# Split SiLU gate, 16 tiles through one core: fifteen stores moved from ScalarE's DMA queue to GpSimd's, with eight rows in one packet

## The chip, the cores and the metric

The kernel runs on one core of one Trainium2 chip. The metric is device time in microseconds (us) of the program; lower is better. The core has one set of 16 DMA engines, which move all data between device memory and the on-chip buffer, and five instruction engines, of which this kernel uses four: ScalarE (ACT in the profile), VectorE (DVE), GpSimd (POOL) and SyncE (SP). TensorE does nothing here.

## The reference

The input has 32 x 512 rows of 2048 float32. Each row is cut in two halves; the first half goes through SiLU and is multiplied by the second.

```python
def reference(x):
    half_dim = x.shape[-1] // 2
    x1, x2 = x[..., :half_dim], x[..., half_dim:]
    silu_x1 = x1 * (1 / (1 + np.exp(-x1)))
    return (silu_x1 * x2).astype(np.float32)
```

So 134.22 MB are read, 67.11 MB are written, and each output element needs one activation and one product.

## The kernel before

The 16384 rows are cut into 16 tiles. A tile is 128 partitions times K = 8 rows of 2048 numbers, so a partition holds 64 KB of input (one contiguous stretch of memory) and 32 KB of output. Each of the 16 DMA engines serves 8 partitions of a tile. In the trace, a load of one tile is therefore 8 packets of 65,536 bytes on each engine, and a store of one tile 8 packets of 32,768 bytes on each engine. The text calls such a packet a row of the engine.

There are two input buffers (`in_pool`, tile `xt`) and two output buffers (`out_pool`, tile `ot`). The order of the instructions is written out by hand; no scheduler moves them.

- `load(i)` (L82) is issued by SP on its DMA queue, which the profile calls q1. `load(0)` and `load(1)` come first. `load(i + 2)` is written after the work of tile i, and has to wait until the product of tile i has read the buffer that it will overwrite.
- For tiles 0 to 14, ScalarE computes SiLU into `ot` (L86) and VectorE multiplies `ot` by the second half of `xt` (L93). Tile 0 is worked in four pieces of two columns (`KC_EDGE`), tiles 1 to 14 in one piece each.
- The store of a tile (L112) is issued by ScalarE on its own DMA queue, which the profile calls q10, once the product is done. For tile 0 it is five transfers, cut by partitions and columns (`OPENING`); for tiles 1 to 14 it is one.
- Tile 15 is worked in two halves (`KS`), each with its own SiLU and product, and its two half stores (L120) are issued by ScalarE.

SiLU of tile i writes the output buffer that tile i - 2 used, so it has to wait until the store of tile i - 2 has landed.

Of the kernel before, what the change touches and what calls it, by code (L numbers as in the profile page):

```python
# [1 line left out]

# [4 lines left out]


def issue_ahead_of_the_first_barrier(nc):

    head, body = nc.main_func.blocks[:2]
    load = next(ins for ins in body.instructions if type(ins).__name__ == "InstDMACopy")
    at = next(
        j for j, ins in enumerate(head.instructions)
        if ins.engine == load.engine and type(ins).__name__ == "InstDrain"
    )
    body.instructions = [ins for ins in body.instructions if ins.name != load.name]  # L20
    head.instructions = head.instructions[:at] + [load] + head.instructions[at:]


@with_exitstack
def kernel(
    ctx: ExitStack,
    tc: tile.TileContext,
    x: bass.AP,
    out: bass.AP,
):  # L30

    nc = tc.nc
    P = nc.NUM_PARTITIONS

    x_flat = x.flatten_outer_dims()  # L40
    out_flat = out.flatten_outer_dims()
    num_rows, in_cols = x_flat.shape
    half = in_cols // 2
    dt = x_flat.dtype

    K = 8
    KC_EDGE = 2
    KS = 4
    OPENING = [
        (slice(0, None, 4), slice(0, 2)),  # L50
        (slice(2, None, 4), slice(0, 4)),
        (slice(2, None, 4), slice(4, None)),
        (slice(0, None, 4), slice(2, None)),
        (slice(1, None, 2), slice(None)),
    ]
    PLAN = [K] * (num_rows // (P * K))

    in_pool = ctx.enter_context(tc.tile_pool(name="in_pool", bufs=2))
    out_pool = ctx.enter_context(tc.tile_pool(name="out_pool", bufs=2))

    plan = []
    row = 0
    for k in PLAN:
        plan.append((row, k))
        row += P * k
    assert row == num_rows
    n_tiles = len(plan)

    def view(flat, i):
        row0, k = plan[i]  # L70
        return flat[row0:row0 + P * k].rearrange("(p k) d -> p k d", k=k)

    nc.at_finalize(issue_ahead_of_the_first_barrier)


    ctx.enter_context(tc.manual_schedule())

    loaded = {}

    def load(i):  # L80
        xt = in_pool.tile([P, K, in_cols], dt, name="xt")
        nc.sync.dma_start(out=xt[:, :plan[i][1], :], in_=view(x_flat, i))  # L82
        loaded[i] = xt

    def silu(ot, xt, c, ce):
        nc.scalar.activation(  # L86
            out=ot[:, c:ce, :],
            in_=xt[:, c:ce, :half],
            func=mybir.ActivationFunctionType.Silu,
        )  # L90

    def mul(ot, xt, c, ce):
        nc.vector.tensor_mul(  # L93
            out=ot[:, c:ce, :],
            in0=ot[:, c:ce, :],
            in1=xt[:, c:ce, half:],
        )

    load(0)
    load(1)  # L100
    for i in range(n_tiles):
        xt = loaded.pop(i)
        ov = view(out_flat, i)
        ot = out_pool.tile([P, K, half], dt, name="ot")
        if i < n_tiles - 1:
            kc = KC_EDGE if i == 0 else K
            for c in range(0, K, kc):
                silu(ot, xt, c, c + kc)
                mul(ot, xt, c, c + kc)

            for ps, ks in OPENING if i == 0 else [(slice(None), slice(None))]:
                nc.scalar.dma_start(out=ov[ps, ks], in_=ot[ps, ks])  # L112
            if i + 2 < n_tiles:
                load(i + 2)
            continue
        for c in range(0, K, KS):
            silu(ot, xt, c, c + KS)
            mul(ot, xt, c, c + KS)
        for c in range(0, K, KS):
            nc.scalar.dma_start(out=ov[:, c:c + KS], in_=ot[:, c:c + KS])  # L120


# [1 line left out]
_INS = ['x']  # L124
_OUTS = [((32, 512, 1024), 'float32')]


# [23 lines left out]
```

## Time and profile before

| | |
|---|---|
| time, median of 3 runs | 470.35 us (470.28, 470.35, 472.34) |
| span of the profiled execution, first to last instruction | 468.4 us |
| that execution's own time | not recorded; the median is 1.95 us over the span |
| VectorE busy | 139.3 us in 20 instructions (30%) |
| ScalarE busy | 114.1 us in 21 instructions (24%) |
| GpSimd busy | 0.2 us in 4 instructions |
| moved by DMA | 201.33 MB at a mean of 430 GB/s |

The page of a profile gives the busy time of each engine, the span cut into 40 slices with the busy share of the 16 DMA engines in each, the DMA queues, and the chain of work that ended last, followed back from the last instruction. Other views list the instructions in order of time, or the busy time in stretches of the span that one chooses. The trace also holds a record of every DMA packet: queue, size, start and duration. "DMA out_dram<-ot" is a store, "DMA xt<-in_x_dram" a load. A DMA "lands" when its last semaphore increment arrives.

### The profile page before, as it was taken

How to read it: one execution, taken by the hardware profiler on the slowest of the kernel's cores; microseconds unless marked ns; L12 is line 12 of the kernel's file. 1: busy time of each engine (PE TensorE's matmuls, PEld its weight loads, DVE VectorE, ACT ScalarE, POOL GpSimd, SP SyncE). 2: the span in 40 equal slices, each digit the busy share in tenths (PEclk: the TensorE clock that was granted, in tenths of full speed). 3: DMA queues.
4: the chain of work that ended last, by engine and by line, in shares of the span. 5: the costliest groups of instructions: out<-in, count | busy, mean ns of one | idle time of the engine just before them, and what ended most of it. 6: DMA issues, size and time to landing. Idle time of an engine off the chain costs nothing.

```text
span 468.4 us, 185 instructions
## 1 busy us (share of the span) xinstructions
DVE 139.3 (30%) x20; ACT 114.1 (24%) x21; POOL 0.2 (0%) x4
## 2 busy tenths in 40 slices
DVE  0070600704207042070520605116061150602543
ACT  1142305005050050601406014060230602306060
POOL 0000000000000000000000000000000000000000
DMA  9899999999999999999999999899999899999998
GB/s 442 364 470 425 448 403 403 493 403 403 448 465 431 403 442 409 493 403 414 437 448 448 403 448 465 386 448 439 411 493 442 372 439 493 403 448 403 428 423 358
DMA packets 4880, 201.33 MB, mean 430 GB/s; under 512 B 592, under 2 KB 592, under 8 KB 592
## 3 DMA queue, kind: packets, MB, share of 16 engines
q1 hardware_dynamic: 2304, 134.22, 66.4%
q10 hardware_dynamic: 2576, 67.11, 33.2%
HBM read 134.22 MB, written 67.11 MB: 430 GB/s over the span
## 4 chain that ended last, share of the span: by engine, by line
DMA 72%; DVE 14%; ACT 11%; DVEq 1%; issue 0%
DMA out_dram<-ot 63%; DVE ot L93 14%; ACT ot L86 11%; DMA xt<-in_x_dram 9%; DVEq L146 1%
## 5 line engine op out<-in xcount | busy, mean ns | idle before, releaser
L93 DVE TENSOR_TENSOR ot<-ot,xt 128x8192 f32<-128x8192 f32 (+2 forms) x20 | 139.3, 6983 | 321.1 <-ACT ot L86 321.1
L86 ACT ACTIVATE ot<-xt 128x8192 f32<-128x8192 f32 (+2 forms) x20 | 112.8, 5661 | 340.2 <-DMA out_dram<-ot 305.8
L86 ACT ACT_TABLE_LOAD x1 | 1.3, 1283 | 0.8 <-PEq L135 0.8
L135 POOL MEMSET const-bfloat16-1.0<- 128x1 bf16 x1 | 0.1, 102 | 0.0
L135 POOL MEMSET const-uint8-127<- 128x1 uint8 x1 | 0.1, 102 | 0.0
L135 POOL MEMSET const-float32-1.0<- 128x1 f32 x1 | 0.1, 99 | 0.0
L135 POOL MEMSET const-float32-0.0<- 128x1 f32 x1 | 0.1, 98 | 0.2 <-issue 0.2
## 6 DMA issues: line engine op xcount, KB each, us to landing
out_dram<-ot ACTq DMA_DIRECT2D x14, 4096.0 KB, 42.2
out_dram<-ot ACTq DMA_DIRECT2D x3, 2048.0 KB, 6.9
out_dram<-ot ACTq DMA_DIRECT2D x2, 512.0 KB, 17.6
out_dram<-ot ACTq DMA_DIRECT2D x1, 768.0 KB, 28.2
xt<-in_x_dram SPq DMA_DIRECT2D x16, 35.1
out_dram<-ot ACTq DMA_DIRECT2D x1, 256.0 KB, 11.3
```

Of the source, the lines that this page charges most:

```text
L86: nc.scalar.activation(out=ot[:, c:ce, :], in_=xt[:, c:ce, :half], func=mybir.ActivationFunctionType.Silu,)
L93: nc.vector.tensor_mul(out=ot[:, c:ce, :], in0=ot[:, c:ce, :], in1=xt[:, c:ce, half:],)
L135: nc = _bacc.Bacc("TRN2", target_bir_lowering=False, num_devices=1)
L146: with _tile.TileContext(nc) as tc:
```

## The change

The stores of tiles 0 to 14 are issued by GpSimd in place of ScalarE, on GpSimd's own DMA queue. Each is one transfer of a whole tile, that of tile 0 too, so that `OPENING` goes. The argument `single_packet=True` asks that what one DMA engine gets of a transfer, here eight rows of 32 KB, be framed as one packet. The loads stay on SP, and the two half stores of tile 15 stay on ScalarE. No tile, buffer or computation changes.

```diff
     KS = 4
-    OPENING = [
-        (slice(0, None, 4), slice(0, 2)),
-        (slice(2, None, 4), slice(0, 4)),
-        (slice(2, None, 4), slice(4, None)),
-        (slice(0, None, 4), slice(2, None)),
-        (slice(1, None, 2), slice(None)),
-    ]
     PLAN = [K] * (num_rows // (P * K))
...
-            for ps, ks in OPENING if i == 0 else [(slice(None), slice(None))]:
-                nc.scalar.dma_start(out=ov[ps, ks], in_=ot[ps, ks])
+            nc.gpsimd.dma_start(out=ov, in_=ot, single_packet=True)
             if i + 2 < n_tiles:
                 load(i + 2)
             continue
```

Instruction by instruction, ScalarE loses 19 DMA issues and keeps 2, GpSimd gains 15 between its start and its end, each of which waits for the product of its tile, and SP's 16 loads stand in the same order with the same waits for the products.

## The prediction

> **What bounds the kernel now.** I read the page's slices and queues first.
>
> ```profile
> DMA  9899999999999999999999999899999899999998
> DMA packets 4880, 201.33 MB, mean 430 GB/s; under 512 B 592, under 2 KB 592, under 8 KB 592
> q1 hardware_dynamic: 2304, 134.22, 66.4%
> q10 hardware_dynamic: 2576, 67.11, 33.2%
> ```
>
> The reader is to see that the 16 DMA engines are busy 66.4% + 33.2% = 99.6% of the span, from the first slice to the last. VectorE (30%) and ScalarE (24%) wait most of the time. Then the chain that ended last:
>
> ```profile
> DMA 72%; DVE 14%; ACT 11%; DVEq 1%; issue 0%
> DMA out_dram<-ot 63%; DVE ot L93 14%; ACT ot L86 11%; DMA xt<-in_x_dram 9%; DVEq L146 1%
> ```
>
> The chain names compute for 25%, but the engines go on moving other tiles while it computes: it is a chain of releases, and the bound is the data. The packet records say the same: 8 rows of a load take 8 x 2.418 = 19.34 us on an engine, 8 rows of a store 8 x 1.213 = 9.70 us, and 16 x 29.04 = 464.7 us of the 468.4 us are rows. First packets start at 1.0 us, the last ends at 467.0 us. So nothing can be won but by shorter rows, and something is lost only where an engine has nothing to move. Where could that be? At the end. There I asked for stretches (columns: stretch, length, DVE, ACT, POOL, clock, DMA share, GB/s) and the order of time:
>
> ```profile
> 410.60:439.60 29.00, 8.69 (x1) 7.03 (x1) 0.00 (x0) 1.00 1.00 434
> 439.60:445.50 5.90, 0.00 (x0) 0.00 (x0) 0.00 (x0) 1.00 1.03 444
> 445.50:448.00 2.50, 0.00 (x0) 0.00 (x0) 0.00 (x0) 1.00 0.97 419
> 448.00:456.10 8.10, 4.44 (x2) 7.12 (x2) 0.00 (x0) 1.00 1.05 453
> ```
>
> ```profile
> 439.57 0.34 ACTq L112 DMA_DIRECT2D out_dram<-ot  x1
> 448.01 7.12 ACT L86 ACTIVATE ot<-xt 128x4096 f32<-128x4096 f32 x2 [17.20 <-DMA out_dram<-ot]
> 451.66 8.76 DVE L93 TENSOR_TENSOR ot<-ot,xt 128x4096 f32<-128x4096 f32 x2 [12.13 <-ACT ot L86]
> 456.12 4.67 ACTq L120 DMA_DIRECT2D out_dram<-ot  x2
> ```
>
> While the last tile is computed (448.0 to 456.1) DMA is full, because stores are late: the last load row of an engine ends at 443.6, and then 3 rows of store 13 and the 8 of store 14 are left, 11 x 1.213 = 13.3 us of work. This backlog hides tile 15's compute. It exists because the two queues take turns: in the packet records each engine alternates one load row, one store row, in a ratio of bytes of 2 to 1, which is that of the whole work, so both queues stay backlogged. Store 14 is issued at 439.57, and its last row ends at 456.9.
>
> **The change, part by part.**
>
> The 19 issues that ScalarE loses (338 to 633 ns each) lie in its idle time: it waits 305.8 us for stores and 34.4 us for loads. Worth nothing. If no queue ran dry, OPENING would be worth nothing either: tile 0's rows carry the same bytes, beside a load that is queued anyway; on an engine 12 rows become 8. The load of tile i + 2 is issued at the same event as before, the end of product i; SP holds no store, so no load moves behind one.
>
> Row length: 65,536 B take 2418 ns, 32,768 B 1213, 16,384 B 611. That is a line with 8 ns per row. If one packet saved all of it, 120 rows x 8 ns = 1.0 us; if rows had to be fetched in another way they could be longer. The nearest row is the trace's third kind of queue (code loading): 8192 B there take 307 ns at best, beside 309 ns on q10, though three of seven take 361 to 549. I take 1213 ns.
>
> The start of a transfer on GpSimd's queue, called d (issue to first row ready), is not in the trace. The nearest rows are 0.87 us (half store issued at 456.12, first row 457.00) and 1.0 us (first load). The low end is 0.87; the high end is unknown, and I carry 5 us, which is what the first store piece took under load (issue 26.02, rows at 31.04), most of it waiting for rows ahead of it. I take 1 to 2.5, nearer the idle rows. [...]
>
> The framing is the part that matters. If an engine takes turns by packet, its turn for a store is now 8 rows (9.70 us) against one load row (2.42): a store, once its turn comes, is done in one go, and the backlog at the end may be gone. The alternation of single rows above is the trace's own evidence for turns. [...]
>
> I follow one engine through this. From the first store (arrived about 26.9, began after the row 28.34 to 31.04, not at 28.34) I read that an engine has its next row chosen when a row starts.
>
> Tile 0: load 0's rows end at 21.0, product 0 at 32.6. Load 1's rows start at 21.0 + 2.42k, so its seventh at 35.5 and its eighth at 37.9. A store arriving before 35.5 (some engines 35.8) goes ahead of the eighth row. It arrives at 32.6 + d: with d below 2.9 it does. Then load 1 ends at 21.0 + 19.3 + 9.7 = 50.1 with store 0 moved.
>
> Tile 1: SiLU starts 0.73 us after the rows' end (21.02 to 21.75) and the product ends 15.8 later (7.03 + 8.69), 16.5 after the load. Load 2's eighth row is chosen at 14.5 and starts at 16.9, so store 1 comes too late for it: load 2 ends 19.3 after load 1, and store 1 goes into the next stretch. Load 3 was issued at 16.5, so engines stay fed.
>
> Tile 2: that stretch holds load 3, store 1 at its start and store 2 (ready at 16.5 + d of a stretch now longer than 29): 38.7 us. Nothing is left over. From there it alternates, 19.3 after odd tiles and 38.7 after even ones, 29.04 on average: same time, engines never idle. The stretch between loads 14 and 15 is a long one: it ends with stores 13 and 14 both moved.
>
> The end: tile 15's load has landed and the store queue is empty. DMA idles until the first half store's rows: 0.73 + 8.11 (448.01 to 456.12: SiLU 3.62, product 4.42, handovers) + 0.87 = 9.7 us. The second half follows 4.34 us after the first, whose rows take 4.9, so there is no second hole. All else is the same rows: 468.4 + 9.7 = 478.1 us of span, and with the 1.95 us around it 480.0 us, against the median of 470.35. The cover that hid 8.1 us of compute is what is lost.
>
> **The rivals.**
>
> *The store of tile 0 misses its place.* If d is over 2.9 us (over 5.3, if an engine chooses later than I read), store 0 goes behind all of load 1. The alternation then has the other phase: stretches after even tiles are short, and load 15 ends with store 14 pending. Store 14 arrives 16.5 + d after load 14; its 9.7 us begin when load 15 ends (19.3) and cover tile 15's compute to 0.0 us. The cost is only d - 2.8 while the engines wait: with d of 3 to 5, 0.2 to 2.2 us, so 470.6 to 472.6. This ends on the other side, not slower by over 0.5%; it decides from d = 2.9 us at one place, 35.5 us into the run. For it: no row here shows how long GpSimd's queue takes. Against it: the idle rows of 0.87 to 1.0, and that one early engine among 16 suffices to hold up load 1.
>
> *The framing does nothing.* If rows still alternate one by one, the backlog stays and so does the time: 470.4, or 469.4 with 1 us off the rows. For it: nothing in the trace shows a packet of several rows.
>
> *The store queue starves the engines at each packet.* If an engine fetches a packet's rows without working meanwhile, each of 15 packets costs up to the 0.87 us of an idle start: 13 us, 493 with the hole at the end. Against it: gaps between rows of different queues are -4 to +2 ns now.
>
> **How the numbers follow.** The hole at the end has 0.62, and its own range is 477.5 to 483 (a hole of 7.5 to 12.5). The missed place has 0.18, the framing without effect 0.09, starving 0.08; 0.03 is left for rows that get shorter in a way that no row here shows. A difference under 0.5% (2.35 us) is about what a measurement of this kernel can't tell from no change. Slower is 0.62 + 0.08 = 0.70, within is 0.27, faster 0.03. The likeliest time is 480.0. For 8 in 10 the range has to reach from the cases without a hole to the top of the hole's own range, with 1 us for d: 470.0 to 484.
>
> **What would show it.** Right: store landings 12 to 16 us after issue where they were 42.2; gaps between load landings of about 19 and 39 in turn; SiLU released by loads and no longer by stores; one empty stretch of 8 to 10 us before the first half store, and slices full before it. The missed place: the same alternation with the short gap last, and store 14 landing after load 15. No effect of framing: landings near 42 and load gaps of 29. Starving: slices of 8 all along. I am wrong altogether if rows of 32,768 B differ from 1213 ns by over 20 ns, for that moves 120 rows on every engine by 2.4 us.

## The result, and the profile after

The changed kernel takes 473.43 us (median of 4 runs, 473.13 to 473.69) against 470.33 us before: a ratio of 1.0059, interval 1.004 to 1.0079, or 3.1 us slower. 480.0 us had been forecast. Medians here are over all executions of a kernel; ratios and intervals leave out a few that ran slow as a whole (one of 12 with five stores on GpSimd at 478.70 us, one of 4 with half loads at 492.56 us, some of the kernel before).

The page after, in the same parts as before:

```profile
span 471.4 us, 174 instructions
DMA  9999999999899999999999899999999999999978
DMA packets 4752, 201.33 MB, mean 427 GB/s; under 512 B 528, under 2 KB 528, under 8 KB 528
q1 hardware_dynamic: 2304, 134.22, 66.0%
q0 software_dynamic: 2160, 62.92, 30.9%
q10 hardware_dynamic: 288, 4.19, 2.1%
```

q0 is GpSimd's queue: its 62.92 MB are the fifteen stores. The DMA engines are as full as before in all slices but the last but one (7 tenths, 9 before). The rows take as long as before: an engine moves rows for 466.6 us on average, 466.4 before, and each row of 32,768 B on q0 takes 1213 ns. So nearly all of the 3.0 us of span is idle time, and the stretches at the end show where (columns as before, DMA share and GB/s last):

```profile
437.90:448.40 10.50, 0.00 (x0) 0.00 (x0) 0.53 (x1) 1.00 0.93 403
448.40:450.80 2.40, 0.00 (x0) 0.01 (x1) 0.00 (x0) 1.00 1.01 437
450.80:456.90 6.10, 2.46 (x1) 6.10 (x2) 0.00 (x0) 1.00 0.98 424
456.90:459.90 3.00, 3.00 (x2) 1.02 (x1) 0.00 (x0) 1.00 0.18 76
459.90:469.70 9.80, 3.30 (x1) 0.00 (x0) 0.00 (x0) 1.00 0.96 405
```

```profile
437.91 0.53 POOL L104 DMA_DIRECT2D out_dram<-ot  x1 [28.39 <-DVE ot L86]
450.79 7.12 ACT L79 ACTIVATE ot<-xt 128x4096 f32<-128x4096 f32 x2 [21.91 <-DMA xt<-in_x_dram]
454.44 8.76 DVE L86 TENSOR_TENSOR ot<-ot,xt 128x4096 f32<-128x4096 f32 x2 [16.83 <-ACT ot L79]
458.90 4.68 ACTq L112 DMA_DIRECT2D out_dram<-ot  x2
```

There is one hole, from 456.9 to 459.9, ahead of the first half store of tile 15. In the packet records of one engine it is 2.98 us long: the last load row ends at 448.45, 7 store rows follow until 456.92, the first row of the half store starts at 459.90. (The mean over the 16 engines is 2.7 us.) Before, 11 store rows followed the last load row, and there was no hole.

The rest of the predicted picture is absent. These are the waits and DMA issues of the changed kernel:

```profile
POOL out_dram L104 <- DVE ot L86: 429.9, 15, 32.6
ACT ot L79 <- DMA xt<-in_x_dram: 343.0, 16, 22.1
out_dram<-ot POOLq DMA_DIRECT2D x15, 4096.0 KB, 34.4
xt<-in_x_dram SPq DMA_DIRECT2D x16, 42.1
```

The same of the kernel before:

```profile
ACT ot L86 <- DMA out_dram<-ot: 305.8, 14, 25.0
out_dram<-ot ACTq DMA_DIRECT2D x14, 4096.0 KB, 42.2
xt<-in_x_dram SPq DMA_DIRECT2D x16, 35.1
```

SiLU now waits for loads (343.0 us) where it waited for stores (305.8), as predicted. But a store takes 34.4 us to land and not 12 to 16, a load 42.1 where it took 35.1, and SiLU starts every 29 us, not after 19 and 39 in turn. Stores are not done in one go. The order of rows on one engine, written out from the packet records (L a load row; S a store row of 32 KB, c of 24, b of 16, a of 8), says so directly:

```
before, from the ninth row       LLLLaLaLLbLbLbLbLLcLcLLSLSSLSLLSLSLSLSLSLSSLSLLSLS ...
before, the end                  ... LLSLSLSLSLSLSSLSLLSLSLSLSLSLSSSSSSSSSSS bbbbbbbbbbbbbbbb
after, from the ninth row        LLLLLLLSLSSLSLSLSLSLSLLSLSSLSLSLSLSLSLLSLSSLSLSLSL ...
after, the end                   ... LLSLSSLSLSLSLSLSLLSLSSLSLSLSLSLSLLSLSSSSSSS bbbbbbbbbbbbbbbb
```

Rows alternate one by one in both kernels. Where two L or two S stand together, the other queue used its turn for the completion (a packet of 4 B, 9 ns) of a transfer: in the kernel before, from 60 us to the last load row, one such packet of the other queue lies between the two rows in all 208 pairs of L and all 208 pairs of S on the 16 engines.

That gives a theory for this kernel. **The lead**: while both queues are backlogged (have rows waiting) they exchange row for row, 64 KB against 32 KB, which is just the ratio of the work (134.22 MB against 67.11), so the distance between them never changes. It is set in the first 60 us and is still there at the end. The four more rows of `OPENING` and its four more completions cost the store queue eight turns; against that its first row starts three load rows earlier (31.0 against 38.8 us), which leaves five. They can be counted at both ends. When load 2's last row ends (the sixteenth L of the orders above), the changed kernel has moved 9 store rows, the kernel before the bytes of 5. When the last load row ends, 11 store rows and two completions are left before, 7 rows and one completion after: four rows and one completion. 7 rows are 8.49 us; from the last load row to the first row of tile 15's store it takes 11.45 us; the hole is the difference, 2.96. **The main rival** was that GpSimd's queue itself costs it: its issues start some 0.3 us after SP's at the same event (33.06 against 32.78 for tile 0), and take 0.53 us instead of 0.36.

### The profile page after: what moved, and what is told of

Same layout as the page of the kernel before. It is cut to its first block, busy times and chain, and to the rows that moved or that the text cites. A ratio compares the mean times of both kernels' runs of the same rounds, so it can differ in the third digit from the quotient of the medians.

```text
span 471.4 us, 174 instructions
## 1 busy us (share of the span) xinstructions
DVE 139.3 (30%) x20; ACT 114.1 (24%) x21; POOL 8.3 (2%) x19
## 3 DMA queue, kind: packets, MB, share of 16 engines
q1 hardware_dynamic: 2304, 134.22, 66.0%
q0 software_dynamic: 2160, 62.92, 30.9%
HBM read 134.22 MB, written 67.11 MB: 427 GB/s over the span
## 4 chain that ended last, share of the span: by engine, by line
DMA 72%; DVE 14%; ACT 11%; DVEq 1%; issue 0%; ACTq 0%
DMA xt<-in_x_dram 72%; DVE ot L86 14%; ACT ot L79 11%; DVEq L138 1%; ACTq L79 0%
## 5 line engine op out<-in xcount | busy, mean ns | idle before, releaser
L79 ACT ACTIVATE ot<-xt 128x8192 f32<-128x8192 f32 (+2 forms) x20 | 112.8, 5661 | 343.0 <-DMA xt<-in_x_dram 343.0
L104 POOL DMA_DIRECT2D out_dram<-ot x15 | 8.1, 540 | 429.9 <-DVE ot L86 429.9
## 6 DMA issues: line engine op xcount, KB each, us to landing
out_dram<-ot POOLq DMA_DIRECT2D x15, 4096.0 KB, 34.4
xt<-in_x_dram SPq DMA_DIRECT2D x16, 42.1
```

The lines of the kernel that those rows point to most:

```text
L79: nc.scalar.activation(out=ot[:, c:ce, :], in_=xt[:, c:ce, :half], func=mybir.ActivationFunctionType.Silu,)
L104: nc.gpsimd.dma_start(out=ov, in_=ot, single_packet=True)
```

## The experiments

**One store for tile 0, on ScalarE's queue.** The kernel before with the opening undone and nothing else:

```diff
-            for ps, ks in OPENING if i == 0 else [(slice(None), slice(None))]:
-                nc.scalar.dma_start(out=ov[ps, ks], in_=ot[ps, ks])
+            nc.scalar.dma_start(out=ov, in_=ot)
```

> The kernel before with the five stores of tile 0 made one, still issued by ScalarE; GpSimd issues nothing. Theory of the lead: each row and each transfer of store 0 costs the store queue one turn, in which a load row gets ahead; with 8 rows and one transfer in place of 12 and five, 7 store rows are left when load 15's rows end, as in the changed kernel, in place of 11, and an engine stands empty before the first half store for 2.5 to 3 us: about 473.2 us. Rival, GpSimd's queue (issues about 0.3 us later, other fetching of rows) costs the 3 us: no hole, 470.3 us.

Measured 473.14 us, ratio 1.0058 (1.004 to 1.0076). GpSimd issues nothing here, and all of the loss is there. 7 rows are left on every engine, and the order of rows is that of the changed kernel, row for row, on all 16.

**Five stores for tile 0, on GpSimd's queue.** The changed kernel's queue and framing with the opening kept:

```diff
             for ps, ks in OPENING if i == 0 else [(slice(None), slice(None))]:
-                nc.scalar.dma_start(out=ov[ps, ks], in_=ot[ps, ks])
+                nc.gpsimd.dma_start(out=ov[ps, ks], in_=ot[ps, ks], single_packet=True)
```

> All stores of tiles 0 to 14 issued by GpSimd in single packets, but tile 0's cut in the five transfers of the kernel before. Theory of the lead: 11 or 12 store rows are left at the end of load 15, no hole, about 470.4 us, with the queue of the changed kernel. Rival, GpSimd's queue: the hole of 2.5 to 3 us stays, about 473.4 us.

Measured 470.88 us, ratio 1.0014 (0.9997 to 1.0031): what GpSimd's queue costs is some 0.5 us by the medians, not clear of nothing, and by the interval at most 1.5 us. 11 rows are left, and the order of rows is that of the kernel before, row for row, on all 16 engines. The same stretch, 457 to 460 us, of these two kernels, first the one with one store on ScalarE, then the one with five on GpSimd:

```profile
457.00:460.00 3.00, 3.00 (x2) 1.88 (x1) 0.00 (x0) 1.00 0.03 11
```

```profile
457.00:460.00 3.00, 3.00 (x1) 0.00 (x0) 0.00 (x0) 1.00 0.94 388
```

The DMA share is 0.03 and 0.94. The two runs together put the 3 us on `OPENING` and take nearly all of them off GpSimd. (The profiled execution of the first is its longest, 474.32 us, with a hole of 3.6 us on average over the engines.)

**The changed kernel without the framing.**

```diff
-            nc.gpsimd.dma_start(out=ov, in_=ot, single_packet=True)
+            nc.gpsimd.dma_start(out=ov, in_=ot)
```

> The changed kernel without the argument for a single packet. If the framing never touches the turns: the same order of rows on every engine, 7 rows left, 473.4 us. If framing costs or saves something: another order of rows or another length of rows, and a time that differs by over 0.3 us.

Measured 473.09 us, ratio 1.0054 (1.0038 to 1.007). The order of rows is that of the changed kernel, row for row, and a row takes 1213 ns. The argument does nothing here that can be measured (473.43 us with it).

**Store 0 in two and in four transfers of full rows.** Neither changes the number or size of rows, so only completions are added.

```diff
-            nc.gpsimd.dma_start(out=ov, in_=ot, single_packet=True)
+            for ps in [slice(j, None, 2) for j in range(2)] if i == 0 else [slice(None)]:
+                nc.gpsimd.dma_start(out=ov[ps], in_=ot[ps], single_packet=True)
```

> The changed kernel with store 0 as two transfers, of the even and of the odd partitions: the same 8 rows of 32 KB on an engine, one completion more. Theory of the lead, with a turn for each completion: 8 rows left in place of 7, the hole shrinks by one row of 1.2 us, to some 1.4 us: about 472.2 us. If only rows take turns and completions do not: 473.4 us.

> The changed kernel with store 0 as four transfers of every fourth partition: the same 8 rows, three completions more. Theory of the lead, with a turn for each completion: 10 rows left (12.1 us), no hole: about 470.4 us. If completions take no turns: 473.4 us.

Two: 472.06 us, ratio 1.0035 (1.0024 to 1.0046), 8 rows left (the profiled execution is a longer one, 472.83 us). Four: 471.15 us, ratio 1.0008 (0.9998 to 1.0018), 9 rows left, and a hole of 0.54 us on average over the engines. The stretch from 457 to 460 us, first with two, then with four:

```profile
457.00:460.00 3.00, 3.00 (x2) 0.58 (x1) 0.00 (x0) 1.00 0.23 98
```

```profile
457.00:460.00 3.00, 3.00 (x2) 0.00 (x0) 0.00 (x0) 1.00 0.82 344
```

In these runs completions take turns, as in the theory: 7, 8 and 9 rows are left with one, two and four transfers. Four was expected to leave 10 rows. All three extra turns are in the packet records, but one of them shows as a completion: when the last load row ends, store 13's completion is left too, which in the changed kernel has already gone by.

**Tile 15 in quarters, in the changed kernel.** `KS` is the number of columns in one piece of tile 15.

```diff
-    KS = 4
+    KS = 2
```

> The changed kernel with tile 15 worked and stored in four quarters in place of two halves. Theory of the lead: 7 rows (8.5 us) are still left when load 15's rows end, but the first part store now comes after 1.9 us of SiLU and 2.3 us of product in place of 3.6 and 4.4, some 3.8 us earlier, so that nothing stands empty: about 470.5 us. Rival, GpSimd's queue costs it somewhere along the run: 473.4 us.

Measured 470.50 us, ratio 1.0000 (0.999 to 1.0011). The lead is not touched (7 rows left), but the first part store comes earlier, and the stretch is full:

```profile
457.00:460.00 3.00, 3.00 (x3) 0.97 (x1) 0.00 (x0) 1.00 0.99 418
```

**Tile 15 in one piece, in the changed kernel**: the same line with `KS = 8`, which makes what has to be covered longer.

> The changed kernel with tile 15 worked and stored in one piece in place of two halves. Theory of the lead: 7 store rows (8.5 us) are left as before, but from the end of the load rows to the first row of tile 15's store it now takes 2.3 us to land and start, 7.03 of SiLU, 8.69 of product and 0.9 of issue, 19.0 us in place of 11.45; the hole grows from 3.0 to 10.5 us: about 481 us. If the 3 us are lost elsewhere along the run and only the chain's own length counts at the end: a hole that does not start at the seventh row's end, and another time.

Measured 480.72 us, ratio 1.0223 (1.0203 to 1.0242). 7 rows of the earlier stores again, and then a hole of 10.3 us on average over the engines:

```profile
457.00:460.00 3.00, 2.22 (x1) 0.75 (x1) 0.00 (x0) 1.00 0.00 0
460.00:470.00 10.00, 6.47 (x1) 0.00 (x0) 0.00 (x0) 1.00 0.37 157
```

Put side by side, the hole is what tile 15 needs, less the rows left (one engine's 11.45 us for halves; 7.6 for quarters, 11.45 - 3.85; 19.0 in one piece, as expected above):

| kernel | rows left, x 1.213 us | needed | hole by this | mean hole in the trace | time, us |
|---|---|---|---|---|---|
| five stores on GpSimd | 11: 13.3 | 11.45 | 0.0 | 0.0 | 470.88 |
| four transfers | 9: 10.9 | 11.45 | 0.5 | 0.54 | 471.15 |
| two transfers | 8: 9.7 | 11.45 | 1.7 | 2.3 | 472.06 |
| changed kernel | 7: 8.5 | 11.45 | 3.0 | 2.7 | 473.43 |
| quarters | 7: 8.5 | 7.6 | 0.0 | 0.0 | 470.50 |
| one piece | 7: 8.5 | 19.0 | 10.5 | 10.3 | 480.72 |

**Neither opening nor GpSimd: ScalarE's single store and quarters.** The first and the quarters' edit together, on the kernel before.

> The kernel before with one store for tile 0, on ScalarE, and tile 15 worked and stored in quarters: neither the opening nor GpSimd. Theory of the lead: 7 rows left, enough for a first quarter store that is ready 3.8 us earlier; no hole: about 470.4 us, the same as the kernel before, and no better, because the rows themselves take what they took.

Measured 470.62 us, ratio 0.9998 (0.9984 to 1.0012). It is as fast as the kernel before and simpler. No version beat the kernel before, in which, with no hole, an engine moves rows for 466.4 of 468.4 us.

**Small rows, with and without the framing.** Each store of tiles 0 to 14 as two transfers of 16 rows of 8 KB on an engine:

```diff
-            nc.gpsimd.dma_start(out=ov, in_=ot, single_packet=True)
+            cut = "p (a b c) d -> p b a (c d)"
+            ovc, otc = ov.rearrange(cut, a=2, b=2), ot.rearrange(cut, a=2, b=2)
+            for b in range(2):
+                nc.gpsimd.dma_start(out=ovc[:, b], in_=otc[:, b], single_packet=True)
```

> The changed kernel with each store of tiles 0 to 14 as two transfers whose rows are 8 KB in place of 32 KB, so that an engine gets 16 rows of 8 KB of each, in a single packet. If the framing is respected for smaller rows: 16 store rows in one go between load rows, stores done early, the store queue empty at the end, a hole of up to 9.7 us, and 3 us more for 24 more rows of 8 ns in each of 15 stores: about 483 us. If it is not respected: single rows of 8 KB alternate with load rows of 64 KB, stores run late, no hole, about 473.3 us.

> The same 8 KB rows without the argument for a single packet. Single rows alternate with load rows, stores run late, no hole; 24 more rows of 8 ns in each of 15 stores add some 2.9 us: about 473.3 us. If it equals the run with the argument in its order of rows, the argument does nothing to the turns.

Measured 538.34 us (ratio 1.1438, 1.1408 to 1.1468) and 538.47 us (1.1438, 1.1417 to 1.1459). On what they were made for, they agree: with the argument and without it, one row of 8 KB goes between two load rows (`LaLaLaLaLaLa`), and there is no group of 16 while load rows wait. In time both missed by 65 us, and the missing piece is a wait that I left out. Waits and one stretch, first without the argument, then with it:

```profile
ACT ot L79 <- DMA out_dram<-ot: 366.0, 14, 51.2
```

```profile
85.50:99.30 13.80, 1.79 (x1) 7.03 (x1) 0.00 (x0) 1.00 1.00 425
99.30:107.40 8.10, 7.04 (x2) 7.03 (x1) 0.90 (x2) 1.00 0.28 90
```

8 KB against 64 KB is far from the ratio of the work, 1 to 2. The loads get through and fill both input buffers, the stores then run alone (85.5 to 99.3), SiLU waits for them since both output buffers are taken, and when they are done nothing is queued on either side until a product ends: a hole of 8.2 us on one engine. There are seven of them in the run, 57 us in all; rows take 12 us longer than in the changed kernel (478.4 against 466.6 us), not 3.

**Loads in rows of 32 KB.** Each load as two transfers of four columns, in the changed kernel and in the kernel before:

```diff
-        nc.sync.dma_start(out=xt[:, :plan[i][1], :], in_=view(x_flat, i))
+        for c in range(0, K, 4):
+            nc.sync.dma_start(out=xt[:, c:c + 4, :], in_=view(x_flat, i)[:, c:c + 4])
```

> The changed kernel with each load as two transfers of four columns, so that a load row is 32 KB like a store row. Theory of the lead: turns now split the bytes 1 to 1, a store is done in about 20 us of alternation, and when load 15's rows end only about 3 rows of store 14 are left (in a stretch of 29 us, store 14 arrives after 17.5 and gets half of the rest, 5.8 of its 9.7 us); the hole is 11.4 - 3.6 = 7.8 us, and 128 more load rows of 8 ns cost 1.0 us: about 479 us, near what was predicted for whole packets. If the backlog at the end is not what counts: 473.4 to 474.4 us.

> The kernel before, with five stores for tile 0 on ScalarE's queue, and the loads cut in the same way. Theory of the lead: the lead that the five small stores give lasts to the end only while both queues stay backlogged; with a split of 1 to 1 the store queue runs empty in every stretch, the lead is forgotten, about 3 rows are left, and it costs the same as with the changed kernel: about 479 us. If the opening's lead lasts anyway: 471.4 us.

Measured 479.37 us (ratio 1.0179, 1.016 to 1.0199) and 474.43 us (1.0084, 1.007 to 1.0098). The part on the lead came true: the store queue runs empty in each period, SiLU starts after some 22 and 36 us in turn in the first and 24 and 34 in the second, and 3 to 4 rows of store 14 are left on most engines in the one, 3 on all in the other, with `OPENING` in the second. In the second run the lead of `OPENING` (11 rows left in the kernel before) is forgotten once the store queue has run dry. The times are not evidence for the size of the hole: with two loads per tile, the first half of tile 15 is computed before the second has landed, which I had overlooked, so less has to be covered. On average over the engines, the holes are 4.7 us in two parts and 2.4 us in one. The second time missed the 479 expected by 4.6 us. That the first agrees with it is chance: an engine's rows take 4.1 us more in all than in the changed kernel (470.7 against 466.6 us), where 1.0 had been expected (below).

## Why the prediction was wrong, point by point

- **The direction and the place**: slower came true, and the one hole is ahead of the first half store, where it was forecast. But its cause is the loss of `OPENING`, and not stores moved in one go as forecast, so the direction is luck.
- **The bound, and where time can be lost**: right. Rows take what they took (466.6 against 466.4 us), the only hole is at the end, and it is what tile 15 needs less the store rows left. With tile 15 in one piece the same sum gave 481 against 480.72 us.
- **The 19 issues of ScalarE, the loads on SP, the row length**: right. 1213 ns, and the order of loads is unchanged. The 1.0 us that one packet might have saved is not there.
- **GpSimd's delay d**: right as far as it can be seen. On one engine store 0's rows start at 38.8 us, after load 1's seventh row (from 35.5) and ahead of its eighth. If an engine chooses its next row when a row starts, as the prediction read it, d was below 2.9; that reading was not tested, and without it the rows only show that d was below 6.2.
- **The framing**: this is the step that failed. "Its turn for a store is now 8 rows" was given 0.62, and nothing in the trace of before showed a packet of several rows. No run shows a turn of eight rows (9.70 us); it was an assumption of mine. The runs show turns of one row (1213 ns at 32 KB), with the argument or without, at 32 and at 8 KB. With that step fall the alternation of 19 and 39 us, the empty store queue at the end, and 9.7 us of hole.
- **"If no queue ran dry, OPENING would be worth nothing either"**: the second step that failed, and the one that hid the true size. No queue did run dry until the loads had ended, and `OPENING` is worth 4 rows of lead (4.9 us), of which the end needs 3 us. I counted its bytes, and what the engine exchanges is turns. So the rival in which the framing does nothing, which is what happened, was priced at 470.4 in place of 473.4.
- **0.73 us from the last load row to SiLU**: mis-sized. It is 2.34 us (448.45 to 450.79): on that engine the completion of load 15 comes behind a store row, at 449.66, and SiLU starts after the last of the load's 16 semaphore increments, which arrive from 450.02 to 450.69. So tile 15 needs 11.45 us and not 9.7. Before, it was much the same (443.6 to a landing at 445.5), but SiLU then waited for store 13 until 448.0.

The packet records of the changed kernel count each row as a packet of its own, although the stores ask for a single one: 1920 packets of 32,768 B on q0, 15 stores x 8 rows x 16 engines. They do not tell whether the argument failed to join the rows, or whether a joined packet was interrupted.

## What to carry to other kernels

In these runs, two DMA queues that are both backlogged share an engine by rows and completions, not by bytes: one load row of 64 KB went against one store row, whether that had 32 KB or 8. The sizes of the rows decided which queue got ahead: with store rows of 8 KB the loads did (538.34 us), with load rows of 32 KB the stores, whose queue ran empty in each period (479.37 us). The lead lasted until one queue ran dry: with `OPENING`, 11 rows were left where none did and 3 where one did. Before an opening is tidied up, count what is still queued when the last load lands, and compare it with the time that the last tile needs to its first store. If it falls short, cutting the last tile finer costs less thought than a lead built up at the start (470.50 us for quarters, 470.88 for five first stores, both on GpSimd's queue).

## What the hardware showed that I had not expected

- In these runs a transfer's completion takes a turn of its own: one more transfer with the same rows moved the end by about one row of 1.213 us (473.43 to 472.06 us).
- An argument that asks for a single packet made no group of rows on GpSimd's queue: at 32 KB the order is the same row for row, and at 8 KB single rows still alternate with load rows (473.43 against 473.09 us, 538.34 against 538.47).
- When store 0 arrives, the load row under way is stretched once, to 3300 ns from 2418 on one engine (3251 to 3587 over the engines of the changed kernel). This is so for the single store on ScalarE's queue too (3189 to 3420 ns over the engines of that run). With loads cut to 32 KB, where the store queue runs dry in each period, this keeps happening on GpSimd's queue only: load rows took 1229 ns on average against 1219 with ScalarE's, which over 256 rows of an engine is 2.6 us, and store rows 1217.7 against 1213.1. The cause was not separated.
